# A decoder step on one core: the pool branch in another order, operands at other offsets in SBUF

## The chip, the cores and the metric

The kernel runs on one core of a Trainium2 chip. The metric is device time in microseconds of one execution. Of the kernel before there are three timed runs, and one execution was recorded by the hardware profiler.

## What is computed

One layer of a decoder for a prompt of 2048 tokens and, beside it, 8 sample sequences of 4 tokens (32 rows), all in fp32, width 1024:

```python
proj = xn @ lp['w_in']                       # gMLP u|v, pool input, memory queries, 3 gates
u, v = jnp.split(jax.nn.gelu(a_part), 2, axis=-1)
vn = layernorm(v, lp['gmlp_ln_g'], lp['gmlp_ln_b'])
sg = chunk_spatial(vn.reshape(B, T, A_GROUPS, A_GDIM), lp['w_spatial'], lp['b_spatial']).reshape(B, T, A_WIDTH)
br_a = (u * sg) @ lp['w_branch_a']
pooled = multi_scale_pool(xb_ext.reshape(B, POOL_STATE + T, B_GROUPS, B_GDIM), n_prev)
mixed = jnp.einsum('btgd,gde->btge', pooled, lp['w_pool']) * lp['pool_scale'].reshape(B_GROUPS, B_GDIM)
br_b = mixed.reshape(B, T, B_WIDTH) @ lp['w_branch_b']
br_c = cross_attn(q, mem_k, mem_v).reshape(B, T, C_WIDTH) @ lp['w_branch_c']
gates = jax.nn.sigmoid((g_part + lp['b_gate']).astype(jnp.float32)).astype(xn.dtype).reshape(B, T, N_BRANCH, D_MODEL)
merged = gates[:, :, 0] * br_a + gates[:, :, 1] * br_b + gates[:, :, 2] * br_c
...
g, u = jnp.split(hn @ lp['w_up'], 2, axis=-1)   # conv_ffn: causal conv of width 3 on g
y = (jax.nn.gelu(c) * u) @ lp['w_down']
```

The sample rows attend to a cache of their own (`cache_mem_k`, `cache_mem_v`, 256 entries for each sequence) and carry states of the pool and of the convolution, which are outputs too.

## The kernel before, in words

Every fp32 operand is split in a high and a low part (`split_half`, lines 113 and 114: ACT rounds, DVE subtracts), and a product is three matmuls: high by high, high by low, low by high. Large products go by a scheme of seven block products in place of eight. Line 392 (`product`) is the heart of it: a weight factor `u` is loaded into PE, and a left factor (`xs`, `xa`, or `X` in the feed-forward stage) streams through, 256, 272 or 512 columns at a time. Lines 136 to 138 (`tok_mm`) are the other way round: a left factor is the weight, 512 columns of `u` stream. Lines 131 to 133 (`mtile`) stream the branches' results `brA` and `brB`.

The prompt is worked on in four blocks of 512 tokens; block 1 also carries the 32 sample rows, so that its tiles have 272 columns in place of 256 and 544 in place of 512. For each block `mixer(b, X, steps)` does, in the order of the program: v by `tok_mm`; in block 0 the constants (`stage_consts`: transposes of gate vectors, spatial weights and conv state); the pool input by line 392, added up in `E` (line 684); the layer norm of v (`norm_v`, lines 644 to 649); sliding means of `E` into `po` (`pool_mean`, lines 578 to 595); the queries; the pool matmul (line 729); the attention to memory, interleaved with the products for u; the spatial gate (line 818); in block 1 the samples' attention (`sample_attn`, lines 939 to 980, one piece); then in four column groups `jp` the three gates' products and the branch projections. `mg` is the merged result in two parts, which `outproj` multiplies by `w_out`. Between products `next(steps, None)` does small steps that prepare later work: the next block's left factors, and (`pair_steps`, `pair_cols`, line 231) rows of the feed-forward input `fx`. `ffn_items` deals these steps to blocks 1 to 3 and to `up(0)`. Then `up` and `down_all` do the feed-forward stage for two halves of the tokens; the activations are reloaded by `load_acts` into `a`, and lines 136 to 138 multiply them by `w_down`.

A scheduler orders the instructions of each engine, by priority in the order of the program and by the buffers that come free. SP issues nearly all loads, in order. The pool "big" (`hb`) has 13 buffers of 8704 bytes, each at a multiple of 512 bytes; the weights' ring has 6, each of whose tiles begins 256 bytes past a multiple of 512. Small PSUM tiles come from a pool of three banks (`tp`).

## Time and profile before

| what | value |
| --- | --- |
| timed runs | 2793.3, 2800.13, 2800.8 us, median 2800.13 |
| profiled execution, its time | 2799.83 us |
| profiled execution, its span | 2798.1 us |
| mean granted clock of PE | 0.987 of 2.4 GHz |
| PE busy | 2711.8 us (97%), 16833 matmuls |
| DVE / ACT / POOL busy | 2059.0 / 1261.8 / 247.9 us |

PE is TensorE's matmul side, PEld its weight loads (which overlap with matmuls), DVE is VectorE, ACT ScalarE, POOL GpSimd, SP the engine that issues the loads. A line such as L392 is a line of the kernel's file, and `mm<-xs,u` says that a tile `mm` was made from `xs` and `u`. In a timeline, equal instructions that follow each other are one row with their count (x31); the brackets behind a row say how long the engine was idle before it, and what it waited for. The time of a matmul row is longer than the distance to the next one, since matmuls are pipelined.

### The profile page before, as it was taken

How to read it: one execution, taken by the hardware profiler on the slowest of the kernel's cores; microseconds unless marked ns; L12 is line 12 of the kernel's file. 1: busy time of each engine (PE TensorE's matmuls, PEld its weight loads, DVE VectorE, ACT ScalarE, POOL GpSimd, SP SyncE). 2: the span in 40 equal slices, each digit the busy share in tenths (PEclk: the TensorE clock that was granted, in tenths of full speed). 3: DMA queues.
4: the chain of work that ended last, by engine and by line, in shares of the span. 5: the costliest groups of instructions: out<-in, count | busy, mean ns of one | idle time of the engine just before them, and what ended most of it. 6: DMA issues, size and time to landing. Idle time of an engine off the chain costs nothing.

```text
span 2798.1 us, 45245 instructions
## 1 busy us (share of the span) xinstructions
PE 2711.8 (97%) x16833; PEld 2408.8 (86%) x16833; DVE 2059.0 (74%) x3915; ACT 1261.8 (45%) x2377; POOL 247.9 (9%) x321
## 2 busy tenths in 40 slices
PE   6899999999999999999899999999999999999998
PEld 5799878899889988999778788889999998888887
DVE  7688858478587777877587777767777767768665
ACT  4565546455566565755444433433333343215112
POOL 2022020111002101110101100000000000001001
PEclk9899999999999999999999999999999999999999
DMA  5467634476646674577743522442222245326212
GB/s 196 143 215 235 232 114 138 154 225 200 196 131 210 209 263 133 168 232 225 255 138 116 150 90 83 141 174 85 61 85 84 63 151 176 100 75 207 94 67 93
DMA packets 434927, 427.32 MB, mean 153 GB/s; under 512 B 28182, under 2 KB 365611, under 8 KB 432651
## 3 DMA queue, kind: packets, MB, share of 16 engines
q1 hardware_dynamic: 434706, 424.42, 47.4%
q8 instruction: 133, 2.18, 0.3%
q14 instruction: 88, 0.71, 0.1%
HBM read 328.29 MB, written 96.15 MB: 152 GB/s over the span
## 4 chain that ended last, share of the span: by engine, by line
PE 39%; issue 9%; POOL 1%; DVE 1%; DMA 0%; ACT 0%; SPq 0%; POOLq 0%; DVEq 0%; ACTq 0%
PE mm L392 30%; PE mm L138 3%; PE mm L137 3%; PE mm L136 3%; POOL rs L143 0%; POOL rs L145 0%; PE tp L231 0%; POOL fx L247 0%; DVE Y L1160 0%; DVE X L303 0%; DVE Y L193 0%; DMA fx<-hd 0%; DMA xd<-fx 0%; ACT tp L158 0%; DVE u L114 0%
## 5 line engine op out<-in xcount | busy, mean ns | idle before, releaser
L113 ACT CAST u<-raw 128x512 fp32r<-128x512 f32 x884 | 539.3, 621 | 993.7 <-PE mm L392 387.2
L392 PE MATMUL mm<-X,u 128*128 128x512 f32 (+2 forms) x5544 | 896.0, 322 | 8.2 <-ACT t L410 3.6
L392 PEld LDWEIGHTS mm<-X,u 128*128 128x128 f32 x5544 | 801.0, 189 | 95.6 <-DVE t L451 4.5
L114 DVE TENSOR_TENSOR u<-raw,u 128x512 fp32r<-128x512 f32 x884 | 600.4, 689 | 198.9 <-ACT u L113 189.9
L392 PE MATMUL mm<-xs,u 128*128 128x256 f32 (+1 forms) x4608 | 619.7, 291 | 16.7 <-ACT t L410 6.1
L392 PEld LDWEIGHTS mm<-xs,u 128*128 128x128 f32 x4608 | 583.5, 193 | 36.8 <-ACT u L113 7.9
L1160 DVE TENSOR_TENSOR Y<-Y,mm 128x512 f32<-128x512 f32 x268 | 182.8, 685 | 110.6 <-PE mm L138 109.8
L138 PE MATMUL mm<-u,a 128*128 128x512 f32 x616 | 244.6, 397 | 0.0
L137 PE MATMUL mm<-u,a 128*128 128x512 f32 x616 | 243.5, 395 | 0.0
L136 PE MATMUL mm<-u,a 128*128 128x512 f32 x616 | 241.5, 392 | 0.0
L143 POOL TENSOR_SCALAR rs<-ss 128x1 f32<-128x1 f32 (+2 forms) x57 | 31.3, 550 | 1520.3 <-ACT tp L158 1519.7
L136 PEld LDWEIGHTS mm<-u,a 128*128 128x128 f32 x616 | 117.0, 190 | 26.6
L137 PEld LDWEIGHTS mm<-u,a 128*128 128x128 f32 x616 | 115.7, 188 | 27.0
L138 PEld LDWEIGHTS mm<-u,a 128*128 128x128 f32 x616 | 115.7, 188 | 25.6
L1084 DVE SCALAR_TENSOR_TENSOR d<-gE,vecs,d 128x1024 f32<-128x1024 f32 x88 | 112.5, 1278 | 6.1 <-ACT d L1082 5.6
L113 ACT CAST u<-sm 128x512 fp32r<-128x512 f32 x120 | 74.4, 620 | 88.1 <-PE mm L392 66.3
L247 POOL TENSOR_SCALAR fx<-fx,rt 128x256 f32<-128x256 f32 x64 | 74.4, 1171 | 421.3 <-DMA fx<-hd 266.1
L114 DVE TENSOR_TENSOR u<-sm,u 128x512 fp32r<-128x512 f32 x120 | 82.5, 688 | 39.6 <-ACT u L113 38.8
L392 PE MATMUL mm<-xa,u 128*128 128x256 f32 x768 | 108.8, 293 | 1.8 <-DVE u L114 1.6
L392 PEld LDWEIGHTS mm<-xa,u 128*128 128x128 f32 x768 | 99.3, 197 | 5.7 <-DVE u L114 2.7
L420 DVE TENSOR_TENSOR t<-mm,t 128x256 f32<-128x256 f32 (+2 forms) x130 | 60.9, 468 | 56.7 <-PE mm L392 56.2
L136 PE MATMUL mm<-u,mg 128*128 128x512 f32 x224 | 88.7, 396 | 0.0
(302 smaller groups left out, 3848.8 us busy)
## 6 DMA issues: line engine op xcount, KB each, us to landing
raw<-in_w_in SPq DMA_DIRECT2D x96, 512.0 KB
raw<-ws SPq DMA_DIRECT2D x96, 512.0 KB
raw<-in_w_up SPq DMA_DIRECT2D x88, 512.0 KB
raw<-in_w_down SPq DMA_DIRECT2D x44, 512.0 KB
raw<-in_w_out SPq DMA_DIRECT2D x32, 512.0 KB
md<-fx SPq DMA_DIRECT2D x24, 512.0 KB
raw<-in_w_in SPq DMA_DIRECT2D x48, 256.0 KB
act<-d SPq DMA_DIRECT2D x22, 528.0 KB
```

Of the source, the lines that this page charges most:

```text
L113: S.copy(uv[:, 0], src)
L114: V.tensor_tensor(uv[:, 1], src, uv[:, 0].bitcast(F32), ALU.subtract)
L136: T.matmul(ps, lhsT=lh, rhs=wh, start=first, stop=False)
L137: T.matmul(ps, lhsT=lh, rhs=wl, start=False, stop=False)
L138: T.matmul(ps, lhsT=ll, rhs=wh, start=False, stop=last)
L143: G.tensor_scalar(r[:n], ms, more, EPS, ALU.add, ALU.add)
L247: G.tensor_scalar(part, part, r, None, ALU.mult)
L392: T.matmul(ps, lhsT=u[:, wl, k], rhs=x(k, xl)[:, c0:c0 + n], start=not more and k + i == 0, stop=k + i == 5, skip_group_check=True)
L420: V.tensor_tensor(v7, pc, v, ALU.add)
L1084: V.scalar_tensor_tensor(d[j][:, 0:FSB], gE[j][:, k:k + FSB], cw(k, f), d[j][:, 0:FSB], ALU.mult, ALU.add)
L1160: return V.tensor_tensor(yd, yd, ps, ALU.add)
```

## The change

1. **64 words.** `xtile` gives the mixer's left factors of 256 columns a start 64 words (256 bytes) into their buffer; those of 272 columns are as before. This concerns 4032 of line 392's matmuls (3264 with `xs`, 768 with `xa`).
2. **Widths.** `brA`, `brB` and `mg` are as wide as their block (512, or 544 in block 1) in place of 544 always; `a` and `ar` have rows of 1088 words in place of 1056; a tile of 56 words ahead of the pool "x7" moves that pool's start.
3. **Pool branch.** `norm_v` and the pool matmul stand behind the memory attention, ahead of the spatial gate. The transposes that write the pool states stand behind the queries.
4. **Constants.** `stage_consts` stands behind the pool product of block 0, and its conv state part in block 1.
5. **Samples' attention.** `sample_attn` is a generator, whose pieces are done between the products of the first gates' column group of block 1; its loads are issued two ahead, and the small steps of that column group are left out.
6. **Steps.** Fewer of the feed-forward rows' steps in blocks 1 and 2, more in block 3, and none in the first column group of `up`.

The diff, cut to its core (the pieces that move without change are shown at the place that they leave or that they reach):

```diff
+AC = 1088
...
+    def xtile(w):
+
+        if w > 256:
+            return hb([P, 2, 4, w], name="xs")
+        return hb([P, 64 + 8 * w], name="xs")[:, 64:64 + 8 * w].rearrange("p (s k c) -> p s k c", s=2, k=4)
...
-            X[i] = hb([P, 2, 4, mw[b]], name="xs")
+            X[i] = xtile(mw[b])
...
+        pad = uctx.enter_context(tc.tile_pool(name="pad", bufs=1, side="right"))
+        G.memset(pad.tile([P, 56], F32, name="pad"), 0.0)
...
+        def stage_conv():
+            st = A["state_conv"].rearrange("l b j (f p) -> (l b j f) p", p=P)
...
+            V.tensor_copy(scT.rearrange("p r f -> p (r f)"), t[:, 0:352])
+
+        hal = mc.tile([P, 2, PSTATE], F32, name="hal")
+        G.memset(hal, 0.0)
+        C["hal"] = hal
...
-            if b == 0:
-                stage_consts()
+            if b == 1:
+                stage_conv()
...
-            brB = [hb([P, 2, 2, NTB], name="brB") for _ in range(2)]
+            brB = [hb([P, 2, 2, n_all], name="brB") for _ in range(2)]
...
-            norm_v()
+            if b == 0:
+                stage_consts()
...
-            for i, po in enumerate(pooled):
-                for (c0, n) in subs:
-                    ps = tp()
-                    T.matmul(ps[:, :n], lhsT=C["wpb"][:, i], rhs=po[:, c0:c0 + n], start=True, stop=True)
-                    hi = brB[0][:, 0, i, c0:c0 + n]
-                    S.activation(hi, ps[:, :n], AF.Copy, scale=vecs[:, 112 + i:113 + i])
-                    V.scalar_tensor_tensor(brB[0][:, 1, i, c0:c0 + n], ps[:, :n], vecs[:, 112 + i:113 + i],
-                                           hi.bitcast(F32), ALU.mult, ALU.subtract)
+            for i in range(2):
+                if smp:
+                    t = tp()
+                    sc = w2.tile([P, NTB], F32, name="sc", tag="w2")
+                    V.tensor_copy(win3(sc[:, 0:NS], 8), Es3[i][:, :, 15:19])
+                    T.transpose(t[:NS, 0:P], sc[:, 0:NS], ident)
+                    V.tensor_copy(nps[:NS, i * P:(i + 1) * P], t[:NS, 0:P])
+                if b == NB - 1:
+                    t = tp()
+                    T.transpose(t[:PSTATE, 0:P], Ep[i][:, TB:TB + PSTATE], ident)
+                    V.tensor_copy(npp[:PSTATE, i * P:(i + 1) * P], t[:PSTATE, 0:P])
...
-            brA = [hb([P, 2, 2, NTB], name="brA") for _ in range(2)]
+            brA = [hb([P, 2, 2, n_all], name="brA") for _ in range(2)]
...
+            norm_v()
+            for i, po in enumerate(pooled):
+                for (c0, n) in subs:
+                    ps = tp()
+                    T.matmul(ps[:, :n], lhsT=C["wpb"][:, i], rhs=po[:, c0:c0 + n], start=True, stop=True)
+                    hi = brB[0][:, 0, i, c0:c0 + n]
+                    S.activation(hi, ps[:, :n], AF.Copy, scale=vecs[:, 112 + i:113 + i])
+                    V.scalar_tensor_tensor(brB[0][:, 1, i, c0:c0 + n], ps[:, :n], vecs[:, 112 + i:113 + i],
+                                           hi.bitcast(F32), ALU.mult, ALU.subtract)
...
-            if smp:
-                sample_attn(sw, brB[1])
+            satt = sample_attn(sw, brB[1]) if smp else iter(())
...
-                    next(steps, None)
+                    if not smp or jp:
+                        next(steps, None)
                     gt = [w2.tile([P, NTB], F32, name="gt", tag="w2") for _ in range(2)]
-                    for h, j, *it in pair(1536 + i * D + jp * 256):
+                    for h, j, *it in pair(1536 + i * D + jp * 256, satt):
...
+                for _ in satt:
+                    pass
...
-                mg.append(hb([P, 2, 2, NTB], name="mg"))
+                mg.append(hb([P, 2, 2, n_all], name="mg"))
...
-            for b in range(8):
-                kbv = kbs[b % 2].rearrange("p (a c) -> p a c", a=2)
-                DMA.dma_start(kbv, ck[b])
...
+
+            def score(b):
                 for hp in range(2):
                     T.matmul(sc[:, 0:M], lhsT=sw[:, (2 * b + hp) * P:(2 * b + hp + 1) * P],
                              rhs=kbT[:, hp * M:(hp + 1) * M],
                              start=b + hp == 0, stop=b == 7 and hp == 1)
+
+            for b in range(2):
+                DMA.dma_start(kbs[b], ck[b])
+            yield
+            for b in range(8):
+                if b:
+                    score(b - 1)
+                t = tp()
+                for hp in range(2):
+                    for mt in range(2):
+                        T.transpose(t[:, hp * M + mt * P:hp * M + (mt + 1) * P], kbs[b % 2][:, mt, hp * P:(hp + 1) * P],
+                                    ident)
+                V.tensor_copy(kbT, t)
+                DMA.dma_start(kbs[b % 2], ck[b + 2] if b < 6 else cv[b - 6])
+                yield
+            score(7)
...
+            for _ in range(3):
+                yield
             t = tp()
             for mt in range(2):
                 T.transpose(t[:, mt * P:(mt + 1) * P], pr[:, mt * P:(mt + 1) * P], ident)
             V.tensor_copy(pT, t[:, 0:M])
+            yield
             ao = tp()
             for b in range(8):
-                vbv = kbs[b % 2].rearrange("p (a c) -> p a c", a=2)
-                DMA.dma_start(vbv, cv[b])
                 for hp in range(2):
                     o = (2 * b + hp) * 8
                     for mt in range(2):
-                        T.matmul(ao[:, o:o + 8], lhsT=vbv[:, mt, hp * P:(hp + 1) * P],
+                        T.matmul(ao[:, o:o + 8], lhsT=kbs[b % 2][:, mt, hp * P:(hp + 1) * P],
                                  rhs=pT[:, mt * P + o:mt * P + o + 8], start=mt == 0, stop=mt == 1)
+                if b < 6:
+                    DMA.dma_start(kbs[b % 2], cv[b + 2])
+                yield
...
-        X = {"A": [hb([P, 2, 4, 256], name="xa") for _ in range(4)], 8: hb([P, 2, 4, 256], name="x8")}
+        X = {"A": [xtile(256) for _ in range(4)], 8: xtile(256)}
...
-            ahead = {1: ffn_items(0)[:4], 2: ffn_items(0)[4:], 3: ffn_items(1) + ffn_items(2)[:4]}
+            ahead = {1: ffn_items(0)[:2], 2: ffn_items(0)[2:6], 3: ffn_items(0)[6:] + ffn_items(1) + ffn_items(2)[:2]}
...
-                for _ in range(2):
+                for _ in range(2 if q else 0):
...
-                next(steps, None)
+                if q:
+                    next(steps, None)
...
-        up(0, pair_steps(ffn_items(2)[4:] + ffn_items(3), vecs[:, 114:122], fx), first["X"], first["W"])
+        up(0, pair_steps(ffn_items(2)[2:] + ffn_items(3), vecs[:, 114:122], fx), first["X"], first["W"])
...
-                    t = hb([P, 2, FSB + NS], name="a")
-                    r = load_raw() if s + gidx == 0 else ra.tile([P, FSB + NS], F32, name="ar", tag="ar")
+                    t = hb([P, 2, AC], name="a")
+                    r = load_raw() if s + gidx == 0 else ra.tile([P, AC], F32, name="ar", tag="ar")
```

How it moves instructions, at three places. First DVE in block 2, from the pool input's last additions (`E`) to the sliding mean (`po`); lines 644 to 649 are the norm of v before, 656 to 661 after, and `u` is the split of weights. Before:

```order
L684 TENSOR_TENSOR E<-mm,t_8610 128x256
L649 SCALAR_TENSOR_TENSOR vn<-vn,rs_8723,lnb 128x512
L648 SCALAR_TENSOR_TENSOR vn<-vn,ba,lng 128x512
L646 BN_AGGR ba<-bs 128x2
L688 COPY hal<-E 128x15
L649 SCALAR_TENSOR_TENSOR vn<-vn,rs_8733,lnb 128x512
L684 TENSOR_TENSOR E<-mm,t_8610 128x256
L648 SCALAR_TENSOR_TENSOR vn<-vn,ba,lng 128x512
L578 TENSOR_TENSOR s<-E 128x514
L649 SCALAR_TENSOR_TENSOR vn<-vn,rs_8743,lnb 128x512
L580 TENSOR_TENSOR s<-s 64x512
L591 SCALAR_TENSOR_TENSOR po<-s,E 64x512 x2
```

With the change:

```order
L661 SCALAR_TENSOR_TENSOR vn<-vn,rs_9287,lnb 128x512
L696 TENSOR_TENSOR E<-mm,t_8566 128x256
L115 TENSOR_TENSOR u<-raw,u 128x512
L696 TENSOR_TENSOR E<-mm,t_8566 128x256
L701 COPY hal<-E 128x15
L590 TENSOR_TENSOR s<-E 128x514
L701 COPY hal<-E 128x15
L115 TENSOR_TENSOR u<-raw,u 128x512
L592 TENSOR_TENSOR s<-s 64x512
L696 TENSOR_TENSOR E<-mm,t_8566 128x256
L603 SCALAR_TENSOR_TENSOR po<-s,E 64x512 x2
```

The norm's instructions, save the last one, no longer stand between the additions and the mean; splits of weights stand there instead.

Second PE in block 0, from the end of v's products (`tok_mm`). `wsn`, `wbn` and `vl` are raw constants that are transposed; line 392 is 401 after. Before:

```order
L138 MATMUL mm<-u,xa 128x512
L500 MATMUL tp<-ident,wsn 128x128 x4
L514 MATMUL tp<-ident,wbn 32x32 x4
L392 MATMUL mm<-xa,u 128x256 x12
L392 MATMUL mm<-xs,u 128x256 x2
L392 MATMUL mm<-xa,u 128x256 x4
L392 MATMUL mm<-xs,u 128x256 x10
L392 MATMUL mm<-xa,u 128x256 x32
L392 MATMUL mm<-xs,u 128x256 x12
L392 MATMUL mm<-xa,u 128x256 x2
L392 MATMUL mm<-xs,u 128x256 x12
L729 MATMUL tp<-po,wpb 128x512
```

With the change:

```order
L139 MATMUL mm<-u,xs 128x512
L401 MATMUL mm<-xs,u 128x256 x72
L496 MATMUL tp<-ident,vl 128x122
L514 MATMUL tp<-ident,wsn 128x128 x4
L401 MATMUL mm<-xs,u 128x256 x21
L528 MATMUL tp<-ident,wbn 32x32 x4
L401 MATMUL mm<-xs,u 128x256 x63
L553 MATMUL tp<-ident,xt 128x128 x7
```

The transposes stood ahead of all pool products, and now stand behind 72 of them; the pool matmul of line 729 is no longer in this stretch.

Third PE in block 1, in the samples' attention: transposes of the cached keys (line 954, then 982), scores (957, then 969). Before:

```order
L954 MATMUL tp<-ident,kb_5273 128x128 x8
L392 MATMUL mm<-xs,u 128x272 x2
L957 MATMUL tp<-kb_5274,sw 128x256 x4
L954 MATMUL tp<-ident,kb_5273 128x128 x8
L957 MATMUL tp<-kb_5274,sw 128x256 x4
L954 MATMUL tp<-ident,kb_5273 128x128 x4
L957 MATMUL tp<-kb_5274,sw 128x256 x2
L968 MATMUL tp<-ident,kb_5274 128x128 x2
L977 MATMUL tp<-kb_5274,kb_5273 128x8 x12
L392 MATMUL mm<-xs,u 128x272 x6
```

With the change:

```order
L401 MATMUL mm<-xs,u 128x272 x12
L969 MATMUL tp<-kb_5322,sw 128x256 x2
L982 MATMUL tp<-ident,kb_5321 128x128 x4
L401 MATMUL mm<-xs,u 128x272 x12
L969 MATMUL tp<-kb_5322,sw 128x256 x2
L982 MATMUL tp<-ident,kb_5321 128x128 x4
L401 MATMUL mm<-xs,u 128x272 x12
L969 MATMUL tp<-kb_5322,sw 128x256 x2
L982 MATMUL tp<-ident,kb_5321 128x128 x4
L401 MATMUL mm<-xs,u 128x272 x12
L969 MATMUL tp<-kb_5322,sw 128x256 x2
L401 MATMUL mm<-xs,u 128x272 x36
```

Between the pieces stand twelve products of the first gates, which before stood behind the whole.

## Rows read from the trace of the kernel before

**Rows 1.** The page: the span, the busy line, and one group (line engine op out<-in | busy, mean ns).

```profile
span 2798.1 us, 45245 instructions
...
PE 2711.8 (97%) x16833; PEld 2408.8 (86%) x16833; DVE 2059.0 (74%) x3915; ACT 1261.8 (45%) x2377; POOL 247.9 (9%) x321
...
L392 PE MATMUL mm<-xs,u 128*128 128x256 f32 (+1 forms) x4608 | 619.7, 291 | 16.7 <-ACT t L410 6.1
```

**Rows 2.** Windows: start:end, length, busy us of each engine, granted PE clock, DMA share, GB/s.

```profile
47.00:84.00 37.00, 27.35 (x168) 23.61 (x166) 32.60 (x66) 12.62 (x27) 7.09 (x8) 0.82 0.45 157
412.00:440.00 28.00, 24.47 (x162) 21.86 (x162) 26.43 (x65) 11.84 (x29) 3.23 (x4) 0.94 0.26 78
486.00:516.00 30.00, 23.75 (x120) 19.92 (x119) 10.45 (x22) 6.04 (x15) 1.72 (x4) 0.82 0.53 172
774.00:796.00 22.00, 16.13 (x97) 13.88 (x96) 20.61 (x39) 6.16 (x14) 4.92 (x10) 0.84 0.25 71
1084.00:1106.00 22.00, 18.17 (x135) 16.23 (x134) 21.59 (x44) 8.00 (x15) 3.19 (x7) 1.00 0.34 115
1376.00:1420.00 44.00, 36.60 (x152) 29.19 (x151) 33.43 (x59) 22.08 (x42) 12.41 (x20) 0.92 0.49 151
```

**Rows 3.** PE's timeline, blocks 0, 2, 3: start, us, instruction, [idle before it and releaser].

```profile
65.81 2.05 PE L729 MATMUL tp<-po,wpb 128*128 128x512 f32 x2 [5.31 <-DVE po L595]
...
72.40 2.04 PE L729 MATMUL tp<-po,wpb 128*128 128x512 f32 x2 [2.40 <-DVE po L595]
...
789.28 2.05 PE L729 MATMUL tp<-po,wpb 128*128 128x512 f32 x2 [3.61 <-DVE po L591]
...
1093.67 0.28 PE L700 MATMUL tp<-ident,E 128*15 128x128 f32 x1 [2.86 <-DVE E L684]
```

**Rows 4.** DVE's timeline, block 2.

```profile
784.97 0.74 DVE L648 SCALAR_TENSOR_TENSOR vn<-vn,ba,lng 128x512 f32<-128x512 f32 x1
...
787.73 1.40 DVE L591 SCALAR_TENSOR_TENSOR po<-s,E 64x512 f32<-64x512 f32 x2
```

**Rows 5.** PE's timeline, sample attention of block 1.

```profile
498.31 1.13 PE L957 MATMUL tp<-kb,sw 128*128 128x256 f32 x4 [0.78 <-DVE kb L955]
...
504.06 0.41 PE L968 MATMUL tp<-ident,kb 128*128 128x128 f32 x2 [1.79 <-DVE kb L965]
```

**Rows 6.** PE's timeline, start of the feed-forward stage.

```profile
1385.99 8.11 PE L392 MATMUL mm<-X,u 128*128 128x512 f32 x28 [3.65 <-ACT t L410]
...
1398.73 0.44 PE L231 MATMUL tp<-ident,fx 128*128 128x128 f32 x2 [3.50 <-POOL fx L247]
```

**Rows 7.** PE's timeline: first and last of 47, 81 and 52 matmuls in a row.

```profile
36.15 0.39 PE L137 MATMUL mm<-u,xa 128*128 128x512 f32 x1
...
46.57 0.39 PE L138 MATMUL mm<-u,xa 128*128 128x512 f32 x1
...
353.20 0.39 PE L136 MATMUL mm<-u,mg 128*128 128x512 f32 x1
...
371.71 0.40 PE L138 MATMUL mm<-u,mg 128*128 128x512 f32 x1
...
2400.05 0.40 PE L138 MATMUL mm<-u,a 128*128 128x512 f32 x1
...
2411.95 0.40 PE L138 MATMUL mm<-u,a 128*128 128x512 f32 x1
```

**Rows 8.** PE's timeline in three stretches, and PEld's groups in the first two.

```profile
1261.77 9.16 PE L392 MATMUL mm<-xs,u 128*128 128x256 f32 x75
...
2259.48 5.94 PE L392 MATMUL mm<-X,u 128*128 128x256 f32 x49
...
624.52 10.24 PE L392 MATMUL mm<-xs,u 128*128 128x272 f32 x79
...
L392 PEld LDWEIGHTS mm<-xs,u 128*128 128x128 f32 x73 | 8.8, 192 | 0.0
...
L392 PEld LDWEIGHTS mm<-X,u 128*128 128x128 f32 x48 | 5.7, 188 | 0.0
```

More of the change, by code (lines that the diff above doesn't have):

```diff
@@ L464, in decoder_step @@
         C = {}
+        def stage_conv():
+            st = A["state_conv"].rearrange("l b j (f p) -> (l b j f) p", p=P)
+            sl_ = w4.tile([P, D], F32, name="stc", tag="w4")
+            t = tp()
+            for i, (r0, rn) in enumerate(((0, 128), (128, 128), (256, 96))):
+                DMA.dma_start(sl_[:rn, i * P:(i + 1) * P], st[r0:r0 + rn])
+                T.transpose(t[:, r0:r0 + rn], sl_[:rn, i * P:(i + 1) * P], ident[:rn, :rn])
+            V.tensor_copy(scT.rearrange("p r f -> p (r f)"), t[:, 0:352])
+        hal = mc.tile([P, 2, PSTATE], F32, name="hal")
+        G.memset(hal, 0.0)
+        C["hal"] = hal
         def stage_consts():
@@ L476, in stage_consts @@
             V.tensor_scalar(vb, t[:, 0:24], 0.5, None, ALU.mult)
-            st = A["state_conv"].rearrange("l b j (f p) -> (l b j f) p", p=P)
-            sl_ = w4.tile([P, D], F32, name="stc", tag="w4")
-            t = tp()
-            for i, (r0, rn) in enumerate(((0, 128), (128, 128), (256, 96))):
-                DMA.dma_start(sl_[:rn, i * P:(i + 1) * P], st[r0:r0 + rn])
-                T.transpose(t[:, r0:r0 + rn], sl_[:rn, i * P:(i + 1) * P], ident[:rn, :rn])
-            V.tensor_copy(scT.rearrange("p r f -> p (r f)"), t[:, 0:352])
             lng = row_bcast(mc, A["gmlp_ln_g"], "lng")
@@ L523, in stage_consts @@
             DMA.dma_start(icnt, A["icnt"])
-            hal = mc.tile([P, 2, PSTATE], F32, name="hal")
-            G.memset(hal, 0.0)
             post_row = row_bcast(mc, A["norm_mix_post"], "post_row")
-            C.update(lng=lng, lnb=lnb, bsp=bsp, wsT=wsT, wbd=wbd, wpb=wpb, icnt=icnt, hal=hal, post_row=post_row)
+            C.update(lng=lng, lnb=lnb, bsp=bsp, wsT=wsT, wbd=wbd, wpb=wpb, icnt=icnt, post_row=post_row)
         def stage_mem():
@@ L692, in mixer @@
                     pool_mean(Es3[i], i, 8, 19, win3(po[:, TB:NTB], 8), False)
-                    t = tp()
-                    sc = w2.tile([P, NTB], F32, name="sc", tag="w2")
-                    V.tensor_copy(win3(sc[:, 0:NS], 8), Es3[i][:, :, 15:19])
-                    T.transpose(t[:NS, 0:P], sc[:, 0:NS], ident)
-                    V.tensor_copy(nps[:NS, i * P:(i + 1) * P], t[:NS, 0:P])
-                if b == NB - 1:
-                    t = tp()
-                    T.transpose(t[:PSTATE, 0:P], E[:, TB:TB + PSTATE], ident)
-                    V.tensor_copy(npp[:PSTATE, i * P:(i + 1) * P], t[:PSTATE, 0:P])
-                pooled.append(po)
-            if smp:
-                for bb in range(8):
-                    DMA.dma_start(O["new_pool_sample"][0, bb, 11:15], nps[4 * bb:4 * bb + 4, 0:BW])
-            if b == NB - 1:
-                DMA.dma_start(O["new_pool_prompt"][0, 0], npp[:PSTATE, 0:BW])
+                pooled.append(po)
             qq = hb([P, 2, 2, NTB], name="qq")
@@ L725, in mixer @@
             qT = [(qq[:, 0, i], qq[:, 1, i]) for i in range(2)]
-            for i, po in enumerate(pooled):
-                for (c0, n) in subs:
-                    ps = tp()
-                    T.matmul(ps[:, :n], lhsT=C["wpb"][:, i], rhs=po[:, c0:c0 + n], start=True, stop=True)
-                    hi = brB[0][:, 0, i, c0:c0 + n]
-                    S.activation(hi, ps[:, :n], AF.Copy, scale=vecs[:, 112 + i:113 + i])
-                    V.scalar_tensor_tensor(brB[0][:, 1, i, c0:c0 + n], ps[:, :n], vecs[:, 112 + i:113 + i],
-                                           hi.bitcast(F32), ALU.mult, ALU.subtract)
+            for i in range(2):
[9 more added lines that the diff above has]
+                    V.tensor_copy(npp[:PSTATE, i * P:(i + 1) * P], t[:PSTATE, 0:P])
+            if smp:
+                for bb in range(8):
+                    DMA.dma_start(O["new_pool_sample"][0, bb, 11:15], nps[4 * bb:4 * bb + 4, 0:BW])
+            if b == NB - 1:
+                DMA.dma_start(O["new_pool_prompt"][0, 0], npp[:PSTATE, 0:BW])
             if b == 0:
@@ L944, in sample_attn @@
             kb3 = w4.tile([P, D], F32, name="kb3", tag="w4")
-            kbs = [kb2[:, 0:512], kb2[:, 512:D]]
+            kbs = [kb2[:, 0:512].rearrange("p (a c) -> p a c", a=2), kb2[:, 512:D].rearrange("p (a c) -> p a c", a=2)]
             kbT, pr, pT = kb3[:, 0:512], kb3[:, 512:768], kb3[:, 0:256]
             sc = tp()
-            for b in range(8):
-                kbv = kbs[b % 2].rearrange("p (a c) -> p a c", a=2)
-                DMA.dma_start(kbv, ck[b])
-                t = tp()
-                for hp in range(2):
-                    for mt in range(2):
-                        T.transpose(t[:, hp * M + mt * P:hp * M + (mt + 1) * P], kbv[:, mt, hp * P:(hp + 1) * P], ident)
-                V.tensor_copy(kbT, t)
+            def score(b):
                 for hp in range(2):
```

2 lines of the change are left out of this document (1 added, 1 removed).

## The prediction, made before the changed kernel was run

> **What bounds the kernel.** I read the page's busy line first: TensorE (PE) is busy for 2711.8 us of a span of 2798.1, or 97%, and the next engine, DVE, for 74% [rows 1]. So only two things can shorten this kernel: stretches in which PE stands still or runs at a lower clock, and the time that one matmul takes when nothing is waited for. Then I read the table of windows [rows 2] for the stretches that the change touches: for each it gives the window's length, PE's busy time and the granted clock. What is missing to the full length is idle time; a clock of 0.82 says that part of the stretch ran at 1.2 GHz instead of 2.4. Then PE's timeline inside those windows says what ended each idle stretch, and the last two groups give the pace of matmuls that wait for nothing. The profiled execution took 2799.83 us, 0.3 below the median of the three runs (2800.13), which lie between 2793.3 and 2800.8; so 0.3% (8.4 us) is about what a measurement of this kernel can tell from no change.
>
> **The waits that the change removes.** In every block PE comes to the pool matmul (line 729) before DVE has made its operand `po`: 5.31 and 2.40 us in block 0, 3.61 in block 2, and 2.86 for `E`, one step earlier in the same chain, in block 3 [rows 3]. DVE is late because the norm of v stands between the pool's own steps: in block 2 its row of 0.74 us at 784.97 lies ahead of `po`'s at 787.73 [rows 4], and five more of its kind stand in the seven us before. The change puts that norm and the pool matmul behind the memory attention (first and second order listing), so the chain to `po` is shorter and nobody waits for it soon.
>
> - Block 0: window 47 to 84 lost 37.00 - 27.35 = 9.65 us idle, and at a clock of 0.82 up to another 0.18 x 37 = 6.7 [rows 2]. Against that stands a new wait: the transposes of the constants, which were done early, now follow 72 pool products, and the constants' loads are issued later on SP, behind a 512 KB weight load; and what is moved to the memory stage may be waited for there. I put that give-back at half of the 16.4, and take **-8** (ends 0 and -14).
> - Block 1: window 412 to 440 lost 3.53 idle and 0.06 x 28 = 1.7 of clock; the pool state's transposes and the norm leave it. I take **-4** of the 5.2.
> - Block 2: window 774 to 796 lost 5.87 and 0.16 x 22 = 3.5. I take **-8** of the 9.4.
> - Block 3: window 1084 to 1106 lost 3.83 at full clock. I take **-3.5**, the wait of 2.86 and the small ones beside it.
> - Sample attention (block 1): in window 486 to 516 PE lost 6.25 idle and 0.18 x 30 = 5.4 of clock, because scores, transposes and the exponentials follow each other directly: 0.78 for a copy, 1.79 for the softmax [rows 5]. Afterwards twelve gate products stand between two steps (third listing), some 1.5 us of work at the pace below, which covers waits of that size. I take **-8** of the 11.6 and leave the rest for the 16 loads of k and v, which are now issued two ahead but on the same SP queue.
> - Start of the feed-forward stage: two waits, 3.65 and 3.50 [rows 6]. The second ends on `fx` from POOL, a step of the next rows' preparation; those steps no longer run in the first column group, and earlier blocks take over more of them. The first, on a copy out of PSUM, has no reason to go. I take **-4**: the second wait, and half a microsecond of clock.
>
> Together -35.5. What is displaced costs something: the norm now has to be done before the spatial gate, DVE's load there is higher, and steps of the later rows come into blocks that had none to spare. I put that at +3.5, a tenth, so **-32** (ends -40 and -11, if only a third is realized because the same DVE work is late somewhere else).
>
> **Alignment of 512-column operands.** The matmuls of `tok_mm` (lines 136 to 138) load a left factor as weights and stream 512 columns of `u`. Where both halves of that factor begin on a multiple of 512 bytes (`xa`), those that wait for nothing come every (46.57 - 36.15)/46 = 226.5 ns. For `a` (rows of 1056 words, so that the low half begins 128 bytes off) it is (2411.95 - 2400.05)/51 = 233.3, and for `mg` (rows of 544 words, so 128, 256 and 384 off) (371.71 - 353.20)/80 = 231.4 [rows 7]. The change gives all of them widths that begin aligned (outside block 1), save that the low half of `a` then lies 256 bytes off. Prices: 1848 matmuls with `a` at 6 ns (between 4.9 and 6.8) 11.1 us; 576 with `mg` at 4.9 ns 2.8; 576 with `brA` and `brB`, which there are the streamed operand, as `mg`, 2.8; 132 with the odd `x7` tile at 6 ns 0.8. That is 17.5 at most. That the offset is the cause is inferred from which tiles are slow, not tried, so I take four fifths, **-14** (ends 0 and -17.5).
>
> By the Trainium skill's page "SBUF — State Buffer", section "Specifications (TRN2)", SBUF has 16-byte cachelines, and crossing to a new line is what costs. All these tiles start on multiples of 16 bytes before and after, so by that page the term would be 0 and the sum 2762. The rows' 5 to 7 ns speak against it, but they compare different tiles at different places; it is a rival below.
>
> **The 64 words.** 4032 matmuls of 256 columns read a left factor (`xs` or `xa`) that begins 256 bytes further on. Their pace now: (9.16 - 0.29)/74 = 119.9 ns, with the mean length of one record, 0.29 [rows 1], taken off the end; the 256-column ones of the feed-forward stage come every (5.94 - 0.29)/48 = 117.7, and the mixer's 272-column ones every (10.24 - 0.29)/78 = 127.6 [rows 8]. The columns alone would take 106.7 and 113.3 at 2.4 GHz, so the excess is 13.2, 11.0 and 14.3. The weight load of the first lasts 192 ns and of the second 188 [rows 8]: the best that the shift could give is those 4 ns, -16 us; the row at the feed-forward pace gives 2.2 ns, -8.9; and 272-column tiles, whose halves already lie at mixed offsets, give no gain or even 14.3 - 13.2 = 1.1 ns more, +4.4. I take 1.5 ns, nearest to the feed-forward row but with a discount for the 272-column one: **-6**.
>
> The Trainium skill's page "TensorE: Matmul & The Clock Gate", section "Step-by-step: what each phase is for", gives PE two independent SBUF read ports, one for the moving operand and one for the weight load, so that a load takes nothing from a running matmul. By that the place of the moving operand relative to the weights is indifferent, this term is 0 and the sum 2754. The row of 192 against 188 ns does not agree with it, by 2%.
>
> **Sum.** -32 - 14 - 6 = -52, from 2799.8: **2748 us**. All of it lies on PE, which is the bound; nothing here is hidden.
>
> **Rivals.**
> 1. *The shift frees the weight load fully*: 192 becomes 188 in all 4032, -16 in place of -6: 2738. For it: two groups that differ just so. Against: no group shows it without other differences. Chance 0.20.
> 2. *Offsets are worth nothing* (16-byte lines): 2799.8 - 32 = 2768. For it: the slow tiles are also those that are freshly written. Chance 0.10.
> 3. *The waits only move*: DVE and SP have the same work, and norm or constants are waited for at their new place; a third is realized: 2799.8 - 11 - 14 - 6 = 2769. Chance 0.12.
> 4. *The waits move and the offsets are worth nothing*, with the shift at +4: 2799.8 - 11 + 4 = 2793, not to be told from no change. Chance 0.07.
> 5. *Slower: the shift makes moving read and weight load meet.* The weights in the ring begin 256 bytes past a multiple of 512, and the moving tiles now as well, where so far they began at different places. If each of the 4032 matmuls then pays a second excess of 14.3 ns, that is +57.7: 2799.8 - 32 - 14 + 57.7 = 2812. It decides from 46/4032 = 11.4 ns on. Against it: the tiles of the feed-forward matmuls begin at eight offsets by their shapes, 256 among them, and these are the faster ones. Chance 0.05.
>
> **How the numbers follow.** My forecast has the remaining 0.46, with a range of its own from 2734 (waits -40, offsets -17.5, shift -8) to 2767 (waits -25, offsets -8, no shift). The range 2722 to 2782 reaches over rivals 1 (2738 with the same spread downwards), 2 and 3, and leaves out 4, 5 and the tails. Faster by over 0.3%: forecast and rivals 1 to 3, 0.88. Within: rival 4, 0.07. Slower: rival 5, 0.05.
>
> **What would show it.** In the profile after: no idle time before the pool matmul in any block, the windows of rows 2 at a clock above 0.95; the sample attention's matmuls with products between them and no wait above 0.5 us; `a` and `mg` at 227 to 229 ns; the mixer's 256-column matmuls at 118.4 ns with loads of 188 to 191. A wait over 5 us before the constants' transposes in block 0, or before the spatial gate in every block, would be rival 3; a pace above 130 ns in the mixer rival 5. The prediction is wrong if the pace of the 256-column matmuls changes by more than 4 ns either way, since 4032 of them turn one nanosecond into 4 us.

## The result and the profile after

The changed kernel takes 2749.06 us (median of 4, 2746.44 to 2751.31) against 2800.3 us: a ratio of 0.9822 (95% interval 0.9804 to 0.9841), so 50 us less, where 52 were forecast. The profiled execution took 2751.31 us. Its page begins:

```profile
span 2749.6 us, 45219 instructions
...
PE 2678.7 (97%) x16833; PEld 2397.1 (87%) x16833; DVE 2057.6 (75%) x3915; ACT 1261.7 (46%) x2377; POOL 252.1 (9%) x322
```

TensorE (PE) is still the bound with 97%; 33 us less of busy time, and 15.4 us less of the time in which it stands still (2749.6 - 2678.7 = 70.9 against 86.3, [rows 1]). Windows of the stretches of [rows 2], laid where the same work now runs (length, busy us of each engine, granted clock, DMA share, GB/s):

```profile
47.00:84.00 37.00, 30.37 (x192) 25.60 (x191) 33.00 (x68) 9.32 (x23) 6.81 (x14) 0.91 0.43 139
405.00:433.00 28.00, 26.53 (x197) 24.12 (x196) 27.05 (x67) 15.20 (x40) 1.42 (x2) 1.00 0.37 113
486.00:516.00 30.00, 29.47 (x233) 29.09 (x234) 15.23 (x33) 13.97 (x30) 0.86 (x2) 1.00 0.61 188
758.00:780.00 22.00, 21.38 (x169) 19.84 (x168) 21.04 (x44) 13.20 (x31) 1.57 (x4) 1.00 0.51 160
1046.00:1068.00 22.00, 18.64 (x141) 18.15 (x139) 20.63 (x41) 10.56 (x21) 4.23 (x7) 0.92 0.45 149
1341.00:1385.00 44.00, 38.60 (x160) 31.12 (x159) 36.41 (x61) 21.71 (x41) 12.22 (x18) 0.92 0.37 120
```

The third is the samples' attention: 0.5 us idle where 6.25 were, at full clock. The fourth, block 2's pool branch, lost 5.87 us and now 0.6. But the first (block 0), the fifth (block 3) and the last (start of the feed-forward stage) still lose 6.6, 3.4 and 5.4 us, at a clock of 0.91 or 0.92. PE's timeline says on what (start, us, instruction, [idle before it and releaser]):

```profile
63.21 1.83 PE L401 MATMUL mm<-xs,u 128*128 128x256 f32 x6 [5.02 <-ACT u L114]
...
1059.56 8.72 PE L401 MATMUL mm<-xs,u 128*128 128x256 f32 x60 [3.02 <-DVE E L696]
...
1335.99 19.48 PE L401 MATMUL mm<-X,u 128*128 128x512 f32 x84
1360.86 19.14 PE L401 MATMUL mm<-X,u 128*128 128x512 f32 x72 [5.40 <-DVE gE L1111]
```

The pool matmul (now line 822) waits for nothing in any block; in blocks 0 and 2 its waits of [rows 3] are gone (in block 1 it had none before either). Here it is in blocks 0 and 2:

```profile
132.19 1.88 PE L822 MATMUL tp<-po,wpb 128*128 128x512 f32 x4
...
801.53 1.02 PE L822 MATMUL tp<-po,wpb 128*128 128x512 f32 x2
```

Both waits of [rows 6] are gone too: the feed-forward stage begins with 84 matmuls in a row. But other waits of the same order stand elsewhere: in block 0 5.02 us for the queries' weights; in block 3 3.02 for `E`, as before, only that a product waits for it now and not a transpose; in the feed-forward stage 5.40 behind the 84 matmuls, until DVE has copied a PSUM bank out into `gE`. That copy stands on DVE behind the last block's rows `mix` and a split of `X`; that their place is the cause was not tried:

```profile
1356.20 1.41 DVE L939 SCALAR_TENSOR_TENSOR mix<-mix,rs,post_row 128x512 f32<-128x512 f32 x2 [1.74 <-POOL rs L146]
1357.53 1.29 DVE L940 TENSOR_TENSOR mix<-mix,xr 128x512 f32<-128x512 f32 x2
1358.73 1.22 DVE L304 TENSOR_TENSOR X<-X 128x1024 fp32r<-128x1024 f32 x1
...
1360.04 1.27 DVE L1111 TENSOR_TENSOR gE<-mm,t 128x512 f32<-128x512 f32 x2
```

The cause of the wait in block 0 is in the timelines of DVE and ACT:

```profile
58.71 0.71 DVE L595 TENSOR_TENSOR s<-E 128x526 f32<-128x526 f32 x1
59.33 0.69 DVE L372 TENSOR_TENSOR sm<-raw 128x512 f32<-128x512 f32 x1
59.94 0.70 DVE L597 TENSOR_TENSOR s<-s 128x524 f32<-128x524 f32 x1
60.55 0.69 DVE L373 TENSOR_TENSOR raw<-raw 128x512 f32<-128x512 f32 x1
...
61.76 0.68 DVE L374 TENSOR_TENSOR sm<-raw 128x512 f32<-128x512 f32 x1
```

```profile
62.54 0.62 ACT L114 CAST u<-sm 128x512 fp32r<-128x512 f32 x1 [3.89 <-DVE sm L374]
```

In block 0 DVE forms the sums of the weights itself (lines 372 to 374). They alternate with the sliding means (595 to 599), and ACT waits 3.89 us for the last one, PE for ACT.

Of the paces, the one of `a` in [rows 7] is now (2361.15 - 2349.59)/51 = 226.7 ns, and the mixer's 256-column matmuls of [rows 8] have not changed. Their means over the whole trace, from the distances between neighbours that wait for nothing (those that are less than 30 ns above the columns divided by 2.4 GHz):

| matmuls, columns | before | after |
| --- | --- | --- |
| `a`, 512 | 232.1 | 227.0 |
| `mg`, 512 | 231.6 | 227.8 |
| `brA` / `brB`, 512 | 232.8 / 232.2 | 228.6 / 226.9 |
| `X` (with x7), 512 | 228.1 | 227.2 |
| `xs`, 256 | 119.8 | 119.8 |

The first and the last matmul of that stretch with `a`:

```profile
2349.59 0.39 PE L138 MATMUL mm<-u,a 128*128 128x512 f32 x1
...
2361.15 0.39 PE L138 MATMUL mm<-u,a 128*128 128x512 f32 x1
```

And the time by stage, from the first matmul of one to that of the next (v's products; memory attention; output projection; product with `w_down`), in us, of the profiles of before, after and the experiments (described below) that do one part alone:

```
                      before  after  widths reorder  satt  steps  satt_steps
first matmul to v      11.7   10.6    10.6    10.5   11.5   10.4    11.7
block 0, v to attention 87.6   78.8    86.9    79.6   86.9   87.6    85.3
  attention to output  223.8  227.5   224.7   228.8  223.7  223.7   224.1
  output to next v      44.6   44.0    43.7    44.6   44.6   44.6    44.6
block 1, v to attention 64.6   59.7    64.8    61.1   64.8   64.6    64.8
  attention to output  258.1  243.0   258.2   257.5  242.7  257.0   242.4
  output to next v      47.8   47.8    47.8    47.8   52.3   47.7    47.8
block 2, v to attention 58.8   50.1    58.7    49.4   59.5   58.4    58.5
  attention to output  213.9  215.2   213.1   216.4  213.7  213.8   214.2
  output to next v      44.5   43.7    43.7    44.5   44.5   44.5    44.5
block 3, v to attention 47.3   45.9    48.2    46.1   47.3   48.2    48.2
  attention to output  219.5  221.4   219.8   220.0  220.9  222.3   219.7
output to w_down       959.7  955.4   957.8   959.7  963.4  959.4   958.4
w_down to the end      503.1  493.5   493.5   503.1  503.0  503.0   503.0
first to last matmul  2785.0 2736.5  2771.3  2769.1 2778.8 2785.1  2767.2
```

A second profile of the changed kernel (the run `again` below) has the same stages within 1.3 us, save block 3's second, which takes 218.8 us there for 221.4 here. A difference of that size between two columns says nothing by itself.

### The profile page after: what moved, and what is told of

It is laid out like the page before. It is cut to its first block, busy times and chain, and to the rows that moved or that the text cites. A ratio compares the mean times of both kernels' runs of the same rounds, so it can differ in the third digit from the quotient of the medians.

```text
span 2749.6 us, 45219 instructions
## 1 busy us (share of the span) xinstructions
PE 2678.7 (97%) x16833; PEld 2397.1 (87%) x16833; DVE 2057.6 (75%) x3915; ACT 1261.7 (46%) x2377; POOL 252.1 (9%) x322
## 4 chain that ended last, share of the span: by engine, by line
PE 73%; issue 11%; DVE 6%; DMA 4%; ACT 3%; POOL 2%; SPq 0%; DVEq 0%; POOLq 0%; ACTq 0%
PE mm L401 48%; PE mm L137 5%; PE mm L138 5%; PE mm L139 4%; PE mm L132 2%; PE mm L133 2%; PE mm L134 2%; DVE u L115 1%; POOL rs L144 1%; ACT tp L159 1%; PE tp L232 1%; DMA raw<-ws 1%; ACT u L114 1%; POOL rs L146 1%; DMA X<-xf 1%
## 5 line engine op out<-in xcount | busy, mean ns | idle before, releaser
L401 PE MATMUL mm<-xs,u 128*128 128x256 f32 (+1 forms) x5376 | 708.9, 290 | 24.2 <-ACT u L114 7.3
L401 PEld LDWEIGHTS mm<-xs,u 128*128 128x128 f32 x5376 | 672.7, 193 | 42.6 <-DVE gt L632 12.2
L137 PE MATMUL mm<-u,a 128*128 128x512 f32 x616 | 240.4, 390 | 0.0
L139 PE MATMUL mm<-u,a 128*128 128x512 f32 x616 | 240.1, 390 | 0.0
L138 PE MATMUL mm<-u,a 128*128 128x512 f32 x616 | 239.9, 390 | 0.0
L139 PEld LDWEIGHTS mm<-u,a 128*128 128x128 f32 x616 | 115.7, 188 | 24.2
L137 PEld LDWEIGHTS mm<-u,a 128*128 128x128 f32 x616 | 115.7, 188 | 23.7
L138 PEld LDWEIGHTS mm<-u,a 128*128 128x128 f32 x616 | 115.7, 188 | 23.3
L865 ACT ACTIVATE gt<-gt,vb 128x512 f32<-128x512 f32 (+1 forms) x96 | 70.1, 730 | 39.3 <-DVE gt L632 38.5
L137 PE MATMUL mm<-u,mg 128*128 128x512 f32 x224 | 87.9, 392 | 0.2 <-ACT mix L924 0.2
L138 PE MATMUL mm<-u,mg 128*128 128x512 f32 x224 | 87.5, 391 | 0.0
```

Source lines behind the costliest of these rows:

```text
L137: T.matmul(ps, lhsT=lh, rhs=wh, start=first, stop=False)
L138: T.matmul(ps, lhsT=lh, rhs=wl, start=False, stop=False)
L139: T.matmul(ps, lhsT=ll, rhs=wh, start=False, stop=last)
L401: T.matmul(ps, lhsT=u[:, wl, k], rhs=x(k, xl)[:, c0:c0 + n], start=not more and k + i == 0, stop=k + i == 5, skip_group_check=True)
L865: S.activation(gt[j][:, 0:n_all], gt[j][:, 0:n_all], AF.Tanh, bias=vb[:, r:r + 1], scale=0.5)
```

## Experiments

Every run is timed in the same rounds as the kernel before; ratios are to it. Three of them (s0, s32, a144) alter the changed kernel in one number, and leave the order of every engine as it is, but for neighbouring ACT instructions at one place in a144.

**s0: without the 64 words.**

```diff
-        return hb([P, 64 + 8 * w], name="xs")[:, 64:64 + 8 * w].rearrange("p (s k c) -> p s k c", s=2, k=4)
+        return hb([P, 8 * w], name="xs").rearrange("p (s k c) -> p s k c", s=2, k=4)
```

> The changed kernel with its mixer's 256-column left factors at the start of their buffers again (0 words in place of 64); every engine has the same instructions in the same order. Theory A (a multiple of 256 bytes is as good as one of 512, so that the 64 words do nothing): the mixer's 256-column matmuls stay at 119.8 ns, total as with the 64 words, 2749 us, within 3. Theory B (the forecast's term, 1.5 ns for each of 4032): 6 us slower, 2755. Rival C (the shift frees the weight load, 4 ns each): 2765.

Measured: 2750.61 us, ratio 0.9831 (0.9818 to 0.9845), and the 256-column pace 119.80 ns against 119.81. The ratio alone would leave B open (2755 is 0.984), but the pace decides: theory A holds, the 64 words do nothing to these matmuls.

**s32: 32 words.** The line of s0, with 32 for 64.

> The changed kernel with 32 words (128 bytes) in place of 64; same order on every engine. Theory A (operands that don't begin on a multiple of 256 bytes cost 5 ns per matmul, whichever operand it is): 4032 matmuls of 256 columns at up to 125 ns in place of 119.8, and some 400 of 512 columns in v's products at 232 in place of 228, together up to +22 us, 2771; and 2751 if only the 512-column ones pay. Theory of 16-byte lines (offsets cost nothing as long as they are multiples of 16 bytes): 2749 and 119.8 ns.

Measured: 2749.47 us, 0.9829 (0.9815 to 0.9842). Both theories miss for the 256-column matmuls, which became 1.0 ns faster (118.8). The 512-column products of v, which load `xs` as weights, became slower, as theory A has it: 232.0 ns for 228.4. Their shapes are the same, so it is the start that does it. Some 4 us less and 1.4 more leave a difference that the total does not resolve. One stretch of block 0, first in the changed kernel, then in s0, then in s32, in PE's timeline and PEld's groups; the busy time of the same 84 matmuls falls by 0.09 us, 1.1 ns each, and the weight loads from 192 to 188 ns:

```profile
298.18 10.33 PE L401 MATMUL mm<-xs,u 128*128 128x256 f32 x84
```

```profile
L401 PEld LDWEIGHTS mm<-xs,u 128*128 128x128 f32 x84 | 10.1, 192 | 0.0
```

```profile
296.08 10.33 PE L401 MATMUL mm<-xs,u 128*128 128x256 f32 x84
```

```profile
L401 PEld LDWEIGHTS mm<-xs,u 128*128 128x128 f32 x84 | 10.1, 192 | 0.0
```

```profile
296.50 10.24 PE L401 MATMUL mm<-xs,u 128*128 128x256 f32 x84
```

```profile
L401 PEld LDWEIGHTS mm<-xs,u 128*128 128x128 f32 x84 | 10.0, 188 | 0.0
```

**widths: the kernel before with the widths alone** (part 2 of the change).

```diff
-                mg.append(hb([P, 2, 2, NTB], name="mg"))
+                mg.append(hb([P, 2, 2, n_all], name="mg"))
...
-                    t = hb([P, 2, FSB + NS], name="a")
+                    t = hb([P, 2, AC], name="a")
```

> The kernel before with the widths alone (brA, brB, mg, a, ar, the pad before x7). Theory A: the matmuls with a, mg, brA, brB and x7 come at 227 to 228.5 ns in place of 231.5 to 233, some 3100 of them, -16 us: 2784 of 2800. Theory of 16-byte lines: the pace in the changed kernel came from elsewhere; 2800, and paces as before. The forecast's value: 2786.

Measured: 2784.12 us, 0.9948 (0.9936 to 0.9961): -14.5 us. All paces are those of the table's column "after" (227.0 for `a`, 227.7 for `mg`), with PE's instructions in the order that they had. The product with `w_down` is 9.6 us shorter, the stage ahead of it (with x7) 1.9, the output projections of blocks 0 and 2 0.9 and 0.8. Theory A holds.

**a144: another width of `a`** in the changed kernel.

```diff
-AC = 1088
+AC = 1060
```

> The changed kernel with rows of 1060 words for a, so that a's low half begins 144 bytes past a multiple of 512 and some of the streamed u 224 bytes past; same order. Theory A (all that counts is whether an operand begins on a multiple of 256 bytes): the matmuls with a come at 232 ns as with 128 bytes, +9 us, 2758. A finer rule (multiples of 128, 64 or 32 matter too): above 234 ns, over +13 us. Offsets don't matter: 227 ns, 2749.

Measured: 2756.15 us, 0.9853 (0.984 to 0.9867); the stage of the product with `w_down` takes 498.6 us against 493.5. The mean, 229.7 ns, is neither theory's. Taken apart by the offsets (addresses of the built programs, distances from one matmul to the next): where `u` begins 224 bytes past a multiple of 512, 228.6 to 233.2 ns; where `u` begins at 256 and the weights at 144, 228.0 to 228.5, against 232.3 to 234.0 for 256 and 128 before. So "a multiple of 256 bytes or 5 ns" is no rule: the same weights at 128 cost 5 ns, at 144 about one.

**reorder: the kernel before with the pool branch's order and the constants** (parts 3 and 4).

```diff
-            norm_v()
+            if b == 0:
+                stage_consts()
...
+            norm_v()
+            for i, po in enumerate(pooled):
```

> The kernel before with the pool branch's order alone (norm and pool matmul behind the memory attention, state transposes behind the queries, constants behind the pool product). Theory from the stages of the changed kernel: block 0 -8.9 up to the attention and +3.7 behind it, block 1 -4.8, block 2 -8.7 and +1.3, block 3 -1.5 and +2, and of these some 3 us are the widths': -14, 2786 of 2800. The forecast's terms (-8, -4, -8, -3.5, less displaced work) say -20 to -23. Rival (the waits only move): -5 or less.

Measured: 2784.14 us, 0.9956 (0.9943 to 0.9968): -12.3, with an interval from some -9 to -16, which takes in the theory's -14 and leaves out the rival's -5 and the forecast's -20. The stages say where the rest is: block 0 -8.0 and then +5.0, block 1 -3.5 and -0.6, block 2 -9.4 and +2.5, block 3 -1.2 and +0.5. Part of each plus is only the pool matmul, which moved from the first stage to the second (four matmuls, some 2 us). In block 0 the wait for the queries' weights, as in the changed kernel, keeps the gain small: -3.0 in sum, where the forecast took -8.

**satt: the samples' attention alone** (part 5).

```diff
-            if smp:
-                sample_attn(sw, brB[1])
+            satt = sample_attn(sw, brB[1]) if smp else iter(())
...
-                    next(steps, None)
+                    if not smp or jp:
+                        next(steps, None)
```

> The kernel before with the samples' attention interleaved alone (generator, loads two ahead, no small steps in that column group). Theory: block 1's stretch from the memory attention to the output projection falls from 258 us to 243, as in the changed kernel, so -15 us, 2785 of 2800. Rival (part of those 15 us is due to the pool branch and the dealing of the steps): between -5 and -9, 2791 to 2795; the forecast's term was -8.

Measured: 2789.87 us, 0.9968 (0.9956 to 0.998): -9 us, the rival's number, though its own stretch gained the theory's 15.4. The next stretch lost 4.5: the last of the steps that the column group now leaves out fall among the output projection's matmuls, where PE waits for POOL to make `fx` and the granted clock is 0.97. Before, it took 47.80 us, with PE busy throughout at full clock. A row of PE's timeline in satt, and the next stretch's window in satt and in the kernel before:

```profile
690.52 0.44 PE L231 MATMUL tp<-ident,fx 128*128 128x128 f32 x2 [1.43 <-POOL fx L247]
```

```profile
678.40:730.60 52.20, 50.57 (x299) 45.74 (x297) 30.17 (x51) 28.23 (x51) 5.33 (x6) 0.97 0.76 242
```

```profile
694.70:742.50 47.80, 47.80 (x292) 43.55 (x291) 25.72 (x37) 25.12 (x43) 0.88 (x2) 1.00 0.63 204
```

And the windows of the attention's own stretch, in satt and in the kernel before:

```profile
435.80:678.50 242.70, 240.96 (x1916) 234.60 (x1917) 177.69 (x401) 136.72 (x283) 25.69 (x32) 1.00 0.61 185
```

```profile
436.60:694.70 258.10, 250.17 (x1924) 241.25 (x1925) 181.66 (x414) 139.53 (x291) 30.57 (x35) 0.97 0.61 185
```

PE's idle time in it falls from 7.93 to 1.74 us, and the clock rises from 0.97 to 1.00.

**steps: the dealing of the feed-forward steps alone, and satt_steps: both** (parts 5 and 6).

```diff
-            ahead = {1: ffn_items(0)[:4], 2: ffn_items(0)[4:], 3: ffn_items(1) + ffn_items(2)[:4]}
+            ahead = {1: ffn_items(0)[:2], 2: ffn_items(0)[2:6], 3: ffn_items(0)[6:] + ffn_items(1) + ffn_items(2)[:2]}
```

> The kernel before with the dealing of the feed-forward steps alone. The forecast's term: -4, from the wait of 3.50 at the start of the feed-forward stage. Theory now: the changed kernel has a wait of 5.40 in that place, on a copy out of PSUM, so the gain there is small or none; alone it gives 0 to -2 (block 1 has fewer steps to finish, block 3 more).

> The kernel before with the samples' attention interleaved and the steps dealt anew. Theory: alone, the interleaving gained 15 us in its own stretch but gave back 4.4 in the next one, where the steps that it leaves out were done at once ahead of the output projection (51.37 us of matmuls in 53 against 47.8), and 3.6 in the feed-forward stage; with fewer steps in block 1 that is not given back: -14 to -17, 2783 to 2786, which is more than the two alone add up to. Rival (the two parts only add): -9 to -10, 2790.

Measured: steps 2795.56 us, 0.9994 (0.9985 to 1.0003), no difference that can be told; the interval, -4 to +1 us, just reaches the forecast's -4, but the feed-forward stage up to `w_down` is 0.3 us shorter. Both: 2781.81 us, 0.9941 (0.9928 to 0.9953): -16.5. The two parts alone add up to some -10.6, so they work together: with fewer steps in block 1 the stretch ahead of the output projection is 47.8 again, and block 3's second stretch takes the moved steps without getting longer (219.7 for 219.5; 222.3 in steps, within what two profiles differ by). Satt alone is also 3.7 us longer between output projection and `w_down`: PE is idle there for 19.1 us in place of 16.9, 9.9 of them waiting for `fx` in place of 8.7, and the granted clock is 0.993 in place of 0.995. Why `fx` comes later was not settled.

**again, late_pool, late_norm, best: can what was given back be had?** The changed kernel itself, and three on top of it, each with the one before. late_pool writes the sliding means behind the queries; late_norm keeps the norm of v behind the additions of `E` on DVE; best uses 32 words for the factors 3, 5, 6 and 7.

```diff
+            for i in range(2):
+                V.tensor_copy(C["hal"][:, i], Ep[i][:, TB:TB + PSTATE])
...
             qT = [(qq[:, 0, i], qq[:, 1, i]) for i in range(2)]
+            for i in range(2):
+                E = Ep[i]
+                po = w2.tile([P, NTB], F32, name="po", tag="w2")
+                pool_mean(win3(E, 1), i, 1, PSTATE + TB, win3(po[:, 0:TB], 1), b == 0)
...
-                    V.bn_stats(bs[:n], vv)
+                    with tc.issue_after(last.ins):
+                        V.bn_stats(bs[:n], vv)
...
-            X[i] = xtile(mw[b])
+            X[i] = xtile(mw[b], 32 if i in (3, 5, 6, 7) else 64)
```

> The changed kernel unaltered, as the neighbour on the same chip for the three that follow: 2749, within 3.

> The changed kernel with the sliding means (pool_mean) written behind the queries in place of ahead of them. Theory: the wait of 5.02 us that the changed kernel has in block 0 (for the queries' weights, whose sums stand on DVE behind the sliding mean) is what the reordering gave back there; it goes, -4 to -5, 2744 to 2745; block 3's wait of 3.02 stays. Rival (the weights' loads are late, not DVE): the wait stays, 2749.

> As late_pool, and on DVE the norm of v may not begin before the last addition of E. Theory: block 3's wait of 3.02 us ahead of E (the norm's instructions fill DVE before the additions, although they are written far behind) goes too: -3 more than late_pool, 2741 to 2742. Rival: the norm is then late for the spatial gate, which waits: as late_pool or slower.

> As late_norm, and the factors 3, 5, 6 and 7, which are mostly streamed, begin 32 words into their buffers in place of 64. By the run with 32 words their 256-column matmuls gain 1.0 ns (118.8 for 119.8), some 2200 of them: -2 us more than late_norm, without the 512-column products of v getting slower (228.5).

Measured: again 2749.51 us, 0.9825 (0.9811 to 0.9838); late_pool 2746.16, 0.9812 (0.9798 to 0.9825), not to be told from it; late_norm 2765.84, 0.9878 (0.9865 to 0.9892), 20 us slower than late_pool, so that its rival held; best 2764.23, 0.9872 (0.9858 to 0.9885).

In late_pool the wait for the queries' weights falls from 5.02 to 1.25, so DVE's order was its cause. But a new one of 3.88 follows 16 us later, for the normalized memory rows that DVE makes:

```profile
60.29 9.42 PE L401 MATMUL mm<-xs,u 128*128 128x256 f32 x60 [1.25 <-ACT u L114]
...
75.97 1.94 PE L553 MATMUL tp<-ident,xt 128*128 128x128 f32 x8 [3.88 <-DVE xt L548]
```

In late_norm block 3 runs from v to the attention in 41.5 us for late_pool's 46.1; that wait is gone. In its place block 3's second stretch takes 226.4 for 217.5 and block 1's 256.2 for 242.5, since DVE now does the norm among the attention's copies. In block 1's, PE is idle for 7.5 us in place of 1.5, at a clock of 0.98 in place of 1.00. PE and then DVE there:

```profile
465.32 0.73 PE L824 MATMUL tp<-po,wpb 128*128 128x272 f32 x2 [2.08 <-DVE brB L827]
...
482.48 5.06 PE L401 MATMUL mm<-xs,u 128*128 128x272 f32 x38 [1.58 <-DVE u L115]
```

```profile
462.73 0.75 DVE L662 SCALAR_TENSOR_TENSOR vn<-vn,rs,lnb 128x512 f32<-128x512 f32 x1 [0.35 <-POOL rs L146]
463.40 0.16 DVE L659 BATCH_NORM_AGGREGATE ba<-bs 16x2 f32<-16x6 f32 x1
463.49 0.65 DVE L657 BATCH_NORM_STATS2 bs<-vg 16x6 f32<-16x512 f32 x1
464.07 0.72 DVE L661 SCALAR_TENSOR_TENSOR vg<-vg,ba,lng 16x512 f32<-16x512 f32 x1
464.72 0.16 DVE L659 BATCH_NORM_AGGREGATE ba<-bs 16x2 f32<-16x6 f32 x1
464.81 0.46 DVE L827 SCALAR_TENSOR_TENSOR brB<-tp,vecs,brB 128x272 fp32r<-128x272 f32 x1
```

The copy of line 827, for which PE waits 2.08 us, stands behind five instructions of the norm. In best the streamed factors gain as in s32 (118.9 ns in the mean), which its total does not resolve. No version beats the changed kernel by more than the measurement can tell.

## Why the prediction was right

The time and the sign came out: 2749 for 2748. The terms did not all: alignment came out near its size, the others were off in both directions. Of the signs that the prediction named, the pool matmul has no wait, the samples' attention runs between products, and `a` and `mg` come at 227.0 and 227.8 ns; but three of the six windows are at a clock of 0.91 or 0.92 and not above 0.95, and the mixer's 256-column matmuls stay at 119.8 ns with loads of 192, where 118.4 and 188 to 191 were forecast.

- **Waits, -32.** Measured by the parts: -12.3 (reorder) and -16.5 (attention with steps), together -28.8; the profiles of the two add up to -33.7 between first and last matmul (2785.0 - 2769.1 and 2785.0 - 2767.2). Inside, three terms were mis-sized. The pool branch was put at -23.5 less 3.5, and gave 12.3. In block 0 a new wait came, as the forecast feared, but for other work: not the constants' loads, but DVE's sums of weights, which stand among the sliding means. In block 3 the wait for `E` stayed, with another matmul in line, since a norm that is written later still runs as soon as DVE has time; in late_norm, where it may not, that wait is gone.
- **Samples' attention, -8.** It gave more: the stretch is 15.4 us shorter, more than the 11.6 lost in its window. Idle time is 6.2 of that (7.93 - 1.74), and the clock an estimated 6.7 (granted 0.974 and 1.00 over 258.1 us): some 13 of the 14.6 that the stretch lost came back, where the forecast took 8 of 11.6. In the rest are eight transposes of small steps that are done later (48 before, 40 in satt). Whether the gain is kept depends on part 6, which the forecast costed by the wrong wait (-4 for `fx`).
- **Start of the feed-forward stage.** The step "I take -4: the second wait" failed, and so did "the first, on a copy out of PSUM, has no reason to go". Both are gone, 3.65 and 3.50, but a new one of 5.40 came behind them, on DVE's copy into `gE`. Part 6 brings it: steps and satt_steps have it too, with 5.11 us, and the kernel before has not. The window's idle time fell by 2.0 (from 7.4 to 5.4), and steps alone makes no difference that can be told. Part 6 pays in block 1.
- **Alignment, -14.** Measured -14.5. That the offset is the cause was inferred, and widths and s32 show it. The size is in part luck: the rows gave 17.5, and the fifth that was taken off stood for doubt about the cause, while it was the price that was too high (`a` gained 5.1 ns on average, not 6). The prediction also saw only `a`'s own offset. Nearly half of the matmuls with `a` stream a `u` from a second ring, of four buffers behind `ar`; its tiles began 128 bytes past a multiple of 512 and begin on one now, since `ar` is wider. Before, matmuls with the aligned half of `a` followed each other every 232.6 ns with `u` from there, and every 227.4 with `u` from the ring of six; now it is 227.1 and 227.3. So part of the gain is the streamed operand's.
- **The 16-byte lines.** By the Trainium skill's page "SBUF — State Buffer", section "Specifications (TRN2)", lines have 16 bytes, and crossing to a new one is what costs; by that alone, offsets that are multiples of 16 should not matter. Here they do: 232.1 against 227.0 ns for `a` in widths, with PE's order unchanged. The measurement decides.
- **64 words, -6.** Measured 0: the step "the row at the feed-forward pace gives 2.2 ns" failed. The feed-forward row's pace comes with other offsets (`X` has 528 columns there; most of its 256-column parts begin 64, 128, 192 or 256 bytes past a multiple of 512, and come at 118.1, 119.6, 115.7 and 116.0 ns before), and s32 shows that 128 bytes give a gain where 256 give none. The discount for 272 columns was misread: 127.6 ns is the mean of a stretch with two longer distances in it, and over the whole trace it is 125.9, an excess of 12.6 and not 14.3. Also the fall of the weight load from 192 to 188 ns, which rival 1 priced at 4 ns a matmul, came in s32 and was worth 1.0. The rule that the prediction set beside it, two independent read ports (the Trainium skill, "TensorE: Matmul & The Clock Gate", "Step-by-step: what each phase is for"), gave 0, as measured here; that 32 words are worth 1.0 ns is not told by it.

So the pool branch was put too high by some 8 us and the shift by 6, and the attention and the feed-forward start together (-12, measured -16.5) too low by some 4. These errors cancel in part, and that 2749 lies as near to 2748 as it does is luck. The parts measured alone (14.5, 12.3 and 16.5) add up to 43 of the 50; each has an interval of some 3.5 us either way, so that what is left isn't told from nothing.

## What to carry to other kernels

Where PE is the bound and a wait is removed, ask what the late engine does next: in blocks 0 and 3 DVE's order was the cause each time, and taking one group of its work out of the way brought the next one in line; at the start of the feed-forward stage two waits went and a third came. Interleave a chain of small dependent matmuls with large ones, and see in the same change where the steps go that stood beside it. Where matmuls that wait for nothing differ by some ns between tiles, compare the tiles' offsets in SBUF, of both operands, and see what a tile's width moves behind it: widths that leave 128 bytes over cost some 5 ns for each of 3100 matmuls here.
